# Normalised units of an FFN in small tiles, the row factor half a unit sooner, recurrence constants in the mixer

## The chip, the cores and the metric

The kernel runs on one core of a Trainium2 chip. The metric is the device time of one execution in microseconds (us). Before the change it is 1784.41 us, the median of three runs (1784.16 to 1784.74). A measurement of this kernel repeats to about a tenth of a per cent.

## What is computed

One decoder layer on x of 256 rows (SEQ) by 2048 columns (D_MODEL), in fp32; D_FF is 5632. Two half-step SwiGLU FFNs stand around a token mixer:

```python
def swiglu_ffn(x, w_gate, w_up, w_down):
    return (jax.nn.silu(x @ w_gate) * (x @ w_up)) @ w_down
...
x = x + 0.5 * swiglu_ffn(rms_norm(x, ffn1_norm), ffn1_w_gate, ffn1_w_up, ffn1_w_down)
z = rms_norm(x, mix_norm) @ w_in
...                                  # conv and RG-LRU with a GELU gate; gated short conv
x = x + y @ w_out                    # y: both branches, each RMS-normalised
x = x + 0.5 * swiglu_ffn(rms_norm(x, ffn2_norm), ffn2_w_gate, ffn2_w_up, ffn2_w_down)
return rms_norm(x, final_norm)
```

Of the recurrence only one thing matters here: it needs a vector worked out from the weights alone, a multiple of softplus(-lambda), and halves of two bias vectors.

## The kernel before

**Numbers.** An fp32 product is made of fp32r parts. A tile is split into hi (a cast by ScalarE) and lo (the tile less hi, by VectorE), and TensorE adds hi by hi, lo by hi and hi by lo in PSUM. So each weight tile of 512 rows by 512 columns (in SBUF 128 partitions by 2048) is loaded by SyncE's queue (`load`, L155, its DMA at L164), cast in two pieces of 1024 and subtracted in one of 2048 (`parts_of`, L169), and then multiplied (`multiply`, L194). In `multiply` the products with the hi part of the weights come first, those with lo last. Raw tiles come from the pool `raws` (three buffers) or, with `kept`, from a pool of the FFN in which the tag "kept" has two buffers. All compute is recorded through the class `Engine` (L42), so the profile puts it all under L42, and tiles are told apart by name.

**x.** The rows stay in SBUF as `xres` (two row halves t = 0, 1 of 128 rows). `Norm` (L207) turns x into `xT`, four units u of 512 columns each (the k of a product), with gain and hi/lo parts, but without the factor of each row. `factor` (L237) takes 1/sqrt of the mean square of each row; `rows` (L243) makes of it a tile `bc`, the factor along the free axis, by two matmuls (`pb`) of ones with a diagonal matrix `diag`, for which there is one buffer.

**An FFN** (`ffn`, L383). Its first 512 columns of gate and up are done with the unnormalised units (loop at L443: u = 0 to 3, for each first gate, then up; weights `raw_g` and `raw_u` by name, sums in `ps_g` and `ps_u`), and the row factor is put on afterwards, when `sg` is made (L485 to 488). In the first FFN (`opening`) the transposes of x stand in the same loop, and up to u = 1 the order of each engine is the order in which the code is written (`Engine.pinned`); everywhere else a scheduler orders the instructions of each engine.

In the same loop stand the factor (L473), the rows (L475) and the normalising of the units (L476 to 482). `normalise(u)` (L421) adds the parts of a unit, multiplies by bc into an fp32 copy `v`, casts it to hi and subtracts for lo, giving `x` of that unit (x_0 to x_3 in the text). The copies v of all four units lie in the two "kept" buffers (L417, L418). When unit 1 is done, `seven_of` (L308) makes the sums and differences of blocks of v that the seven-product passes need (tiles `spare` and `xs`).

After that five pairs of 512-column blocks follow (L531), for each pair a gate pass and an up pass (`seven`, L326). Such a pass takes the 2 by 2 blocks of units 0 and 1 with seven products instead of eight (12 matmuls of 512 columns each, `product_of`) and units 2 and 3 in the usual way (`usual`, four blocks of 24 matmuls): 180 matmuls. The first products are product 0 (weight w11 alone, into `ps_g_a`) and product 4 (w12 - w11, into `ps_g_c`, stationary side `xs`); the sum of product 4 is then copied by ScalarE (`s5`), units 2 and 3 go on into the same sum and into `ps_g_e`. Both w11 and w12 are loaded into "kept" buffers (L336). Eight transposes of `sg` (`ph`) stand in the gate pass. After pairs 0, 2 and 4 the down products follow (L493). Tiles of 512 columns that live for a while (`spare`, `sg`, `s1`, `s5` and the like) come from a tag "keep" with 13 buffers (L390).

**Between the FFNs.** In the first FFN `prepare` (L566) is called at L491: it turns the small vectors (gains, biases, convolution weights, lambda) with two transposes (`pv_many`, `pv_conv`) and works out the recurrence's constants with an Abs and an Exp on ScalarE and 25 small VectorE steps (`lam_...`). The mixer (L605) walks through ten blocks of 512 columns of w_in (order at L782, weights `raw_in`, sums `ps_in`) and does its elementwise work piece by piece beside them: `defer` (L59) queues a piece, `pump` (L66) takes some behind each unit. Then comes the product with w_out (L803, weights `raw_o`), and the second FFN.

Of the kernel before, what the change touches and what calls it, by code (L numbers as in the profile page):

```python
# [10 lines left out]
F32 = mybir.dt.float32  # L11
F32R = mybir.dt.float32r
AF = mybir.ActivationFunctionType
ALU = mybir.AluOpType
AX = mybir.AxisListType

P = 128
D = 2048
S = 256
FF = 5632  # L20
NT = S // P
# [4 lines left out]
UK = 4  # L26
# [22 lines left out]
def hybrid_block(ctx: ExitStack, tc: tile.TileContext, a: dict, out: bass.AP):  # L49
    nc = tc.nc  # L50
    Engine.pinned = False
    dve, act, pe = (Engine(tc, e) for e in (nc.vector, nc.scalar, nc.tensor))
    x = a["x"][0]
# [5 lines left out]
    def defer(cost, fn):  # L59
        pending.append((cost, fn))  # L60
# [23 lines left out]
    def f32(ap):  # L84
        return ap.bitcast(F32)
# [104 lines left out]
    def stationary(tile, t):  # L190

        return [(tile[:, j, t * P : (t + 1) * P], tile[:, j, S + t * P : S + (t + 1) * P]) for j in range(UK)]
# [14 lines left out]
    class Norm:  # L207
# [35 lines left out]
        def rows(self):  # L243

            pb = bank(f"pb_{self.name}")
            for t in range(NT):
                dg = work.tile([P, P], F32, tag="diag", name=f"diag_{self.name}_{t}", bufs=1)
                dve.tensor_scalar(dg, ident, self.r[:, t : t + 1], None, op0=ALU.mult)
                pe.matmul(pb[:, t * P : (t + 1) * P], ones, dg, start=True, stop=True)
            self.bc = work.tile([P, S], F32, tag="bc", name=f"bc_{self.name}")  # L250
            dve.tensor_copy(self.bc, pb[:, :S])
# [71 lines left out]
    def quad(tile):  # L323
        return tile.rearrange("p (j c) -> p j c", j=UK)
# [58 lines left out]
    def ffn(tag, norm, after, opening=False):  # L383
        with tc.tile_pool(name=f"ffn{tag}", bufs=1) as fp:
# [29 lines left out]
                    turn_hidden(*waiting.pop(0))  # L414


            vs = [fp.tile([P, UK, 2, S], F32, tag="kept", name=f"v{tag}_{i}", bufs=2) for i in range(2)]  # L417
            vs = [vs[u // 2][:, :, u % 2, :] for u in range(4)]  # L418
            xs, sf = [], {}

            def normalise(u):  # L421

                bcs = norm.bc.unsqueeze(1).to_broadcast([P, UK, S])
                x = f32(norm.xT[u])
                dve.tensor_tensor(vs[u], x[:, :, :S], x[:, :, S:], op=ALU.add)
                dve.tensor_tensor(vs[u], vs[u], bcs, op=ALU.mult)
                xs.append(big(f"x{tag}_{u}"))
                act.copy(xs[u][:, :, :S], vs[u])
                dve.tensor_tensor(xs[u][:, :, S:], vs[u], f32(xs[u][:, :, :S]), op=ALU.subtract)
                if u == 1:  # L430
                    pair = [big(f"xs{tag}_{i}") for i in range(2)]
                    sf.update(
                        seven_of(
                            xs[0], xs[1],
                            {(t, i): vs[i][:, :, t * P : (t + 1) * P] for t in range(NT) for i in range(2)},
                            quad(keep(f"spare{tag}")),
                            [(b[:, :, o : o + P], b[:, :, o + P : o + S]) for b in pair for o in (0, S)],
                        )
                    )
# [3 lines left out]
            for u in range(KD // UK):  # L443
                for m, w in (("g", wg), ("u", wu)):
                    n = f"{m}{tag}_0_{u}"
                    src = w[u * UK * P : (u + 1) * UK * P, :CW]
                    if opening and (u, m) == (0, "g"):
                        pieces = ((0, 1), (1, 2), (2, 4))
                        raw = load(src, n, pieces, lambda i: load_x(1) if i == 1 else None)
                        blk = parts_of(raw, n, pieces, lambda i: norm.turn((i,) if i < 2 else (2, 3)))  # L450
                        for j in range(UK):
                            for t in range(NT):
                                yh, yl = stationary(norm.xT[u], t)[j]
                                pe.matmul(ps[m, t], yh, blk[j][0], start=j == 0, stop=False)
                                pe.matmul(ps[m, t], yl, blk[j][0], start=False, stop=False)
                                pe.matmul(ps[m, t], yh, blk[j][1], start=False, stop=False)
                        continue
                    raw = load(src, n)
                    if opening and u < 2 and m == "u":
                        load_x(u + 2)  # L460
                    blk = parts_of(raw, n, ((0, 2), (2, 4)), (lambda i: None) if opening else None)
                    if opening and u < 3 and m == "u":
                        norm.turn(range(4 * u + 4, 4 * u + 8))
                        if u == 0:
                            norm.squares(0)
                        norm.squares(u + 1)
                    multiply([(ps[m, t], stationary(norm.xT[u], t), u == 0, u == 3) for t in range(NT)], blk)
                    pump(1.5)
                    if (u, m) == (1, "u"):
                        Engine.pinned = False  # L470
                        flush()
                    elif (u, m) == (2, "u") and opening or (u, m) == (2, "g") and not opening:
                        norm.factor()  # L473
                    elif (u, m) == (3, "g") and opening or (u, m) == (2, "u"):
                        norm.rows()  # L475
                        normalise(0)  # L476
                    if u == 3:
                        for k in range(len(xs), len(xs) + 2):
                            if k < 4:
                                normalise(k)  # L480
            for k in range(len(xs), 4):
                normalise(k)
            xs = list(enumerate(xs))[2:]
# [3 lines left out]
                dve.scalar_tensor_tensor(sg, ps["u", t], norm.r[:, t : t + 1], sg, op0=ALU.mult, op1=ALU.mult)  # L487
                waiting.append((0, t, sg, False))
            turn_of["hold"] = False
            if tag == 1:  # L490
                prepare()  # L491

            def down(last):  # L493
                us = sorted(set(hidden) | {w[0] for w in waiting})
# [36 lines left out]
            for s in range(5):  # L531
                cs = (CW + 2 * s * CW, 2 * CW + 2 * s * CW)
                sg = {}

                def total(ps, tiles):
                    for p in tiles[1:]:
                        dve.tensor_tensor(tiles[0], tiles[0], p, op=ALU.add)
                    if not tiles:
                        return ps
                    dve.tensor_tensor(tiles[0], ps, tiles[0], op=ALU.add)  # L540
                    return tiles[0]

                def gate(t, n, ps, tiles):
                    g = total(ps, tiles)
                    sg[t, n] = tiles[0] if tiles else keep(f"z{tag}_{s}")
                    act.activation(sg[t, n], g, AF.Silu)

                def up(t, n, ps, tiles):
                    dve.tensor_tensor(sg[t, n], total(ps, tiles), sg[t, n], op=ALU.mult)
                    if (t, n) == (1, 0):  # L550
                        settle()
                    waiting.append((1 + 2 * s + n, t, sg[t, n], s % 2 == 0))

                seven(wg, (0, 1), cs, sf, xs, f"g{tag}_{s}", keep, gate, settle)
                seven(wu, (0, 1), cs, sf, xs, f"u{tag}_{s}", keep, up)
                if s % 2 == 0:
                    down(s == 4)
            extra.clear()


# [3 lines left out]
    sp2, hba, hbi = small("sp2"), small("hba"), small("hbi")  # L564

    def prepare():  # L566
        for t in turns:
            t()

        lam = vec["lru_lambda"]  # L570
        m, e, den, sr, s2, pl = (small(f"lam_{n}") for n in ("abs", "exp", "den", "s", "s2", "poly"))
        act.activation(m, lam, AF.Abs)
        act.activation(e, m, AF.Exp, scale=-1.0)
        dve.tensor_scalar(den, e, 2.0, None, op0=ALU.add)
        dve.reciprocal(den, den)
        dve.tensor_tensor(sr, e, den, op=ALU.mult)
        dve.tensor_tensor(s2, sr, sr, op=ALU.mult)
        dve.tensor_scalar(pl, s2, 2.0 / 17, 2.0 / 15, op0=ALU.mult, op1=ALU.add)
        for d in (13, 11, 9, 7, 5, 3, 1):
            dve.tensor_tensor(pl, pl, s2, op=ALU.mult)  # L580
            dve.tensor_scalar(pl, pl, 2.0 / d, None, op0=ALU.add)
        dve.tensor_tensor(pl, pl, sr, op=ALU.mult)
        dve.tensor_scalar(sp2, lam, -1.0, 0.0, op0=ALU.mult, op1=ALU.max)
        dve.tensor_tensor(sp2, sp2, pl, op=ALU.add)
        dve.tensor_scalar(sp2, sp2, 2.0, None, op0=ALU.mult)
        dve.tensor_scalar(hba, vec["lru_b_a"], 0.5, None, op0=ALU.mult)
        dve.tensor_scalar(hbi, vec["lru_b_i"], 0.5, None, op0=ALU.mult)
# [17 lines left out]
    with tc.tile_pool(name="mixer", bufs=1) as mp, tc.tile_pool(name="mixw", bufs=2) as mw:  # L605
# [165 lines left out]
        def sc_b(ps, half):  # L771
            if any(4 * half + f not in ys for f in range(4)):
                flush()
            for f in range(4):
# [4 lines left out]
                dve.tensor_tensor(y, b, y, op=ALU.mult)  # L779
                defer(0.8, lambda q=q, y=y: finish(y, NH + q, vec["sc_out_norm"][:, q : q + 1], 1, q == 0))  # L780

        order = [  # L782
            (lru_x, 0, 0), (lru_x, 0, 1), (sc_c, 3, 0), (lru_gate, 1, 0), (sc_x, 4, 0),
            (lru_gate, 1, 1), (sc_c, 3, 1), (sc_x, 4, 1), (sc_b, 2, 0), (sc_b, 2, 1),
# [116 lines left out]
```

## Time and profile before

| what | us |
|---|---|
| median of three runs | 1784.41 |
| the profiled execution, its own time | 1786.55 |
| its span in the profile | 1784.7 |
| TensorE (PE) busy | 1740.5 (98%) |
| VectorE (DVE) busy | 1494.5 (84%) |
| ScalarE (ACT) busy | 1047.0 (59%) |

The profiled execution is one of its own, longer than its span by 1.85 us, and the medians come from other runs. In rows of the timeline, the first number is the start within the span and the second the duration in us (of all instructions of the row together, whose number is at the end, x8); then come engine, line, operation, out<-in, and in brackets the idle time of the engine before it, with what ended that. A row of an `SPq` lists issues of the DMA queue. A row of a stretch gives from:to and its length, then busy time and, in brackets, the number of instructions of TensorE's matmuls, TensorE's weight loads, VectorE, ScalarE and GpSimd, and behind them the granted clock of TensorE (1 is full), the share of DMA and GB/s.

### The profile page before, as it was taken

What the parts mean: (1) busy time and instruction counts of PE and PEld (TensorE: products, weight loads), DVE (VectorE), ACT (ScalarE), POOL (GpSimd) and SP (SyncE); (2) the same over time, 40 slices, a digit from 0 to 9 for tenths busy, and PEclk for the clock granted to TensorE, in tenths of its full rate; (3) what the DMA queues carried; (4) which work ended last, traced back from release to release, by engine and by line L of the source; (5) the groups of instructions that cost most, each with busy time, mean ns of one, the idle gap of its engine ahead of it and who ended that gap; (6) DMA issues with size and microseconds to landing.
All of it is one profiled execution on the core that took longest, in us unless ns stands there. A gap on an engine that the chain in (4) does not pass through costs nothing. (4 is left out here: it accounts for less than half of the span.)

```text
span 1784.7 us, 20306 instructions
## 1 busy us (share of the span) xinstructions
PE 1740.5 (98%) x8031; PEld 1439.8 (81%) x8031; DVE 1494.5 (84%) x1228; ACT 1047.0 (59%) x1342; POOL 6.9 (0%) x32
## 2 busy tenths in 40 slices
PE   8699999999999999999999998999999999999998
PEld 7488788888888888888888886788788888888886
DVE  7798989989789888588987666989899887899895
ACT  6465566665466656565765453665466554566654
POOL 1000000000000000000000000000000000000000
PEclk9899999999999999999999999999999999999999
DMA  8266555574565564555555564564566647555652
GB/s 286 93 208 217 207 194 189 189 240 166 184 205 196 190 234 167 164 188 190 176 186 194 199 204 151 188 224 138 203 216 204 202 158 259 188 189 189 236 179 105
DMA packets 173904, 343.24 MB, mean 192 GB/s; under 512 B 5620, under 2 KB 8048, under 8 KB 173680
## 3 DMA queue, kind: packets, MB, share of 16 engines
q1 hardware_dynamic: 173344, 340.82, 56.9%
q8 instruction: 63, 1.03, 0.2%
q10 hardware_dynamic: 144, 1.05, 0.1%
q14 instruction: 33, 0.27, 0.0%
q0 software_dynamic: 320, 0.07, 0.0%
HBM read 339.82 MB, written 2.10 MB: 192 GB/s over the span
## 5 line engine op out<-in xcount | busy, mean ns | idle before, releaser
L42 PE MATMUL ps_in<-xT_nm,hi_in 128*128 128x512 f32 x640 | 222.9, 393 | 0.0
L42 ACT CAST hi_g_p<-raw_g 128x1024 fp32r<-128x1024 f32 x140 | 142.2, 1049 | 110.6 <-DVE raw_g L42 46.1
L42 DVE TENSOR_TENSOR lo_g_p<-raw_g,hi_g_p 128x2048 fp32r<-128x2048 f32 x70 | 159.7, 2287 | 42.1 <-ACT hi_g_p L42 40.9
L42 ACT CAST hi_u_p<-raw_u 128x1024 fp32r<-128x1024 f32 x140 | 141.3, 1049 | 70.9 <-PE ps_u_a L42 25.7
L42 PE MATMUL ps_in<-xT_nm,lo_in 128*128 128x256 f32 x640 | 178.5, 280 | 0.7 <-DVE lo_in L42 0.7
L42 DVE TENSOR_TENSOR lo_u_p<-raw_u,hi_u_p 128x2048 fp32r<-128x2048 f32 x70 | 159.1, 2286 | 20.3 <-ACT hi_u_p L42 20.1
L42 PE MATMUL ps_d<-hi_d,h 128*128 128x512 f32 x704 | 169.6, 392 | 0.0
L42 PEld LDWEIGHTS ps_d<-hi_d,h 128*128 128x128 f32 x704 | 131.5, 188 | 28.2
L42 PEld LDWEIGHTS ps_in<-xT_nm,hi_in 128*128 128x128 f32 x640 | 119.6, 187 | 26.0
L42 ACT CAST hi_d<-raw_d 128x1024 fp32r<-128x1024 f32 x88 | 88.2, 1049 | 69.2 <-PE ps_u_d L42 22.7
L42 DVE TENSOR_TENSOR lo_d<-raw_d,hi_d 128x2048 fp32r<-128x2048 f32 x44 | 100.6, 2290 | 33.3 <-ACT hi_d L42 33.3
L42 PEld LDWEIGHTS ps_in<-xT_nm,lo_in 128*128 128x128 f32 x640 | 120.6, 189 | 1.6 <-DVE lo_in L42 1.5
L42 DVE TENSOR_TENSOR lo_in<-raw_in,hi_in 128x2048 fp32r<-128x2048 f32 x40 | 91.3, 2284 | 32.5 <-ACT hi_in L42 32.3
L42 ACT CAST hi_in<-raw_in 128x1024 fp32r<-128x1024 f32 x80 | 81.5, 1049 | 61.8 <-PE ps_in L42 48.5
L42 ACT CAST hi_d_p<-raw_d 128x1024 fp32r<-128x1024 f32 x84 | 84.4, 1048 | 56.4 <-DVE raw_d L42 32.9
L42 DVE TENSOR_TENSOR lo_d_p<-raw_d,hi_d_p 128x2048 fp32r<-128x2048 f32 x42 | 95.5, 2287 | 18.0 <-ACT hi_d_p L42 17.9
L42 ACT CAST hi_g_x<-raw_g 128x1024 fp32r<-128x1024 f32 x80 | 81.2, 1049 | 41.6 <-PE ps_g_c L42 22.9
L42 ACT CAST hi_u_x<-raw_u 128x1024 fp32r<-128x1024 f32 x80 | 80.6, 1049 | 37.2 <-PE ps_u_c L42 25.5
L42 DVE TENSOR_TENSOR raw_u<-raw_u,raw_u 128x2048 f32<-128x2048 f32 x40 | 91.6, 2290 | 10.1 <-DMA raw_u<-in_ffn_w_up_dram 9.5
L42 DVE TENSOR_TENSOR raw_g<-raw_g,raw_g 128x2048 f32<-128x2048 f32 x40 | 91.4, 2287 | 7.0 <-DMA raw_g<-in_ffn_w_gate_dram 6.5
L42 DVE TENSOR_TENSOR lo_g_x<-raw_g,hi_g_x 128x2048 fp32r<-128x2048 f32 x40 | 91.4, 2284 | 2.3 <-ACT hi_g_x L42 2.1
L42 DVE TENSOR_TENSOR lo_u_x<-raw_u,hi_u_x 128x2048 fp32r<-128x2048 f32 x40 | 91.4, 2285 | 0.9 <-ACT hi_u_x L42 0.2
(348 smaller groups left out, 3606.9 us busy)
## 6 DMA issues: line engine op xcount, KB each, us to landing
raw_u<-in_ffn_w_up_dram SPq DMA_DIRECT2D x88, 1024.0 KB, 5.2
raw_d<-in_ffn_w_down_dram SPq DMA_DIRECT2D x88, 1024.0 KB, 5.2
raw_g<-in_ffn_w_gate_dram SPq DMA_DIRECT2D x87, 1024.0 KB, 5.3
raw_in<-in_w_in_dram SPq DMA_DIRECT2D x40, 1024.0 KB, 5.1
raw_o<-in_w_out_dram SPq DMA_DIRECT2D x16, 1024.0 KB, 5.1
xres<-in_x_dram SPq DMA_DIRECT2D x4, 512.0 KB, 8.2
fin<-in_final_norm_dram ACTq DMA_DIRECT2D x1, 1024.0 KB, 5.6
out_dram<-xres SPq DMA_DIRECT2D x4, 256.0 KB, 2.7
```

The costliest lines, as they stand in the source:

```text
L42: ins = getattr(self.engine, name)(*args, **kwargs)
```

## The change

Three things, which the diff shows whole.

1. The copies v of the normalised units leave the two "kept" buffers. Each unit and row half has a tile of 512 columns of its own with tag "keep" (eight of its 13 buffers). `normalise` works row half by row half: add, multiply, cast and subtract each take 512 columns twice where they took 1024 once. The "kept" buffers hold nothing but raw weights.
2. The row factor: `diag` has two buffers (the pool's default) instead of one. In the first FFN `factor` is called ahead of up unit 2's products instead of behind them, and `rows` and the normalising of unit 0 behind up unit 2 instead of behind gate unit 3. In the second FFN `factor` is called behind up unit 1 instead of gate unit 2, and `rows` and the normalising of unit 0 behind gate unit 2 instead of up unit 2.
3. `prepare` is not called in the first FFN but queued ahead of the mixer's loop. The two transposes of the small vectors, which stood in it, come behind the up pass of the first FFN's pair s = 1.

```diff
@@ class Norm, rows
-                dg = work.tile([P, P], F32, tag="diag", name=f"diag_{self.name}_{t}", bufs=1)
+                dg = work.tile([P, P], F32, tag="diag", name=f"diag_{self.name}_{t}")
@@ ffn
-            vs = [fp.tile([P, UK, 2, S], F32, tag="kept", name=f"v{tag}_{i}", bufs=2) for i in range(2)]
-            vs = [vs[u // 2][:, :, u % 2, :] for u in range(4)]
-            xs, sf = [], {}
+            xs, vs, sf = [], {}, {}
 
             def normalise(u):
 
-                bcs = norm.bc.unsqueeze(1).to_broadcast([P, UK, S])
-                x = f32(norm.xT[u])
-                dve.tensor_tensor(vs[u], x[:, :, :S], x[:, :, S:], op=ALU.add)
-                dve.tensor_tensor(vs[u], vs[u], bcs, op=ALU.mult)
                 xs.append(big(f"x{tag}_{u}"))
-                act.copy(xs[u][:, :, :S], vs[u])
-                dve.tensor_tensor(xs[u][:, :, S:], vs[u], f32(xs[u][:, :, :S]), op=ALU.subtract)
+                for t in range(NT):
+                    hi, lo = (slice(o + t * P, o + (t + 1) * P) for o in (0, S))
+                    v = vs[t, u] = quad(keep(f"v{tag}_{u}_{t}"))
+                    x = f32(norm.xT[u])
+                    dve.tensor_tensor(v, x[:, :, hi], x[:, :, lo], op=ALU.add)
+                    dve.tensor_tensor(v, v, norm.bc[:, hi].unsqueeze(1).to_broadcast([P, UK, P]), op=ALU.mult)
+                    act.copy(xs[u][:, :, hi], v)
+                    dve.tensor_tensor(xs[u][:, :, lo], v, f32(xs[u][:, :, hi]), op=ALU.subtract)
                 if u == 1:
                     pair = [big(f"xs{tag}_{i}") for i in range(2)]
                     sf.update(
                         seven_of(
                             xs[0], xs[1],
-                            {(t, i): vs[i][:, :, t * P : (t + 1) * P] for t in range(NT) for i in range(2)},
+                            vs,
...
+                        if u == 2:
+                            norm.factor()
                     multiply([(ps[m, t], stationary(norm.xT[u], t), u == 0, u == 3) for t in range(NT)], blk)
                     pump(1.5)
                     if (u, m) == (1, "u"):
                         Engine.pinned = False
                         flush()
-                    elif (u, m) == (2, "u") and opening or (u, m) == (2, "g") and not opening:
-                        norm.factor()
-                    elif (u, m) == (3, "g") and opening or (u, m) == (2, "u"):
+                        if not opening:
+                            norm.factor()
+                    elif (u, m) == (2, "u" if opening else "g"):
                         norm.rows()
                         normalise(0)
...
             turn_of["hold"] = False
-            if tag == 1:
-                prepare()
@@ ffn, loop over s
                 if s % 2 == 0:
                     down(s == 4)
+                elif s == 1 and tag == 1:
+                    for t in turns:
+                        t()
@@ prepare
-        for t in turns:
-            t()
@@ mixer
+        defer(5.0, prepare)
         order = [
```

## The prediction

> **What bounds the kernel now.** The page first, part 2, the clock that TensorE was granted in 40 slices:
>
> ```profile
> PEclk9899999999999999999999999999999999999999
> ```
>
> The chain that ended last is TensorE work, at full clock nearly everywhere. So what counts is where TensorE stands still. The list of its waits (total, times, longest):
>
> ```profile
> PE ps_g_a L42 <- ACT hi_g_p L42: 23.4, 3, 15.0
> PE ps_g_c L42 <- ACT hi_g_p L42: 3.9, 2, 2.1
> ```
>
> 27.3 us go to two tiles, ps_g_a and ps_g_c: the first products of the first seven-product pass of each FFN. TensorE's timeline shows both places (start, duration; the bracket is the idle time before). FFN 1's first gate pass lies between pv_many, which takes the place right behind the last ps_u, and ps_u_a:
>
> ```profile
> 56.66 0.23 PE L42 MATMUL pv_many<-ident,rows_many 80*128 80x80 f32 x1
> ...
> 72.06 3.78 PE L42 MATMUL ps_g_a<-hi_g_p,x 128*128 128x512 f32 x8 [14.97 <-ACT hi_g_p L42]
> ...
> 78.87 3.54 PE L42 MATMUL ps_g_c<-hi_g_p,xs 128*128 128x512 f32 x8 [2.07 <-ACT hi_g_p L42]
> ...
> 120.08 1.98 PE L42 MATMUL ps_u_a<-hi_u_p,x 128*128 128x512 f32 x8
> ```
>
> ```profile
> 1102.55 1.98 PE L42 MATMUL ps_u<-lo_u,xT_n 128*128 128x512 f32 x8
> 1112.70 3.78 PE L42 MATMUL ps_g_a<-hi_g_p,x 128*128 128x512 f32 x8 [8.17 <-ACT hi_g_p L42]
> 1116.28 1.35 PE L42 MATMUL ps_g_a<-lo_g_p,x 128*128 128x512 f32 x4
> 1119.43 3.11 PE L42 MATMUL ps_g_c<-hi_g_p,xs 128*128 128x512 f32 x8 [1.80 <-ACT hi_g_p L42]
> ```
>
> Who is late behind hi_g_p? ScalarE's cast waits for a transfer, and SyncE's issues tell since when:
>
> ```profile
> 70.96 1.99 ACT L42 CAST hi_g_p<-raw_g 128x1024 fp32r<-128x1024 f32 x2 [1.44 <-DMA raw_g<-in_ffn_w_gate_dram]
> ```
>
> ```profile
> 65.84 24.80 SPq L164 DMA_DIRECT2D raw_g<-in_ffn_w_gate_dram  x4
> ```
>
> ```profile
> 1106.47 18.89 SPq L164 DMA_DIRECT2D raw_g<-in_ffn_w_gate_dram  x3
> ```
>
> ```profile
> raw_g<-in_ffn_w_gate_dram SPq DMA_DIRECT2D x87, 1024.0 KB, 5.3
> ```
>
> The weight tile w11 takes a "kept" buffer, and both of these hold the units' fp32 copies until the last is normalised. Its load starts only at 65.84 and 1106.47, takes about 5.3 us (the page's part 6), and the cast follows: normalising, load and cast stand in a row.
>
> A smaller cost is the clock, in stretches of 1 us (the third number from the end):
>
> ```profile
> 62.00:63.00 1.00, 0.00 (x0) 0.00 (x0) 1.00 (x3) 1.00 (x3) 0.00 (x0) 0.56 0.00 0
> 75.00:76.00 1.00, 1.00 (x4) 0.61 (x4) 1.00 (x3) 0.00 (x0) 0.00 (x0) 0.61 0.00 0
> 79.00:80.00 1.00, 1.00 (x3) 0.82 (x4) 1.00 (x2) 1.00 (x2) 0.00 (x0) 0.59 0.00 0
> 82.00:83.00 1.00, 1.00 (x4) 0.78 (x4) 1.00 (x3) 0.56 (x1) 0.00 (x0) 0.70 0.00 0
> ```
>
> TensorE idle from 57 falls to half clock within 62 to 63, is back within 75 to 76, and falls again at about 79.4 after the idle 2.07 us, for some 3.2 us.
>
> A dense pass prices the loss. From the chain of waits:
>
> ```profile
> 1500.36 21.95 PE ps_d L42 x96
> ```
>
> 21.95 / 96 = 0.2286 us per matmul. A first pass has 180 of them (seven products of 12, four usual blocks of 24) and 8 transposes with a quarter of the columns (0.8 us, an estimate between 8 x 0.06 and 8 x 0.23): 41.9 us. FFN 1 took 120.08 - 56.66 = 63.4, a loss of **21.5** (14.97 + 2.07 of waits, the rest clock).
>
> **The change part by part.** VectorE sets the new times, so its rows:
>
> ```profile
> 50.98 0.29 DVE L42 TENSOR_SCALAR diag_n<-ident,r_n 128x128 f32<-128x128 f32 x1 [6.98 <-PE pb_n L42]
> 51.85 0.43 DVE L42 COPY bc_n<-pb_n 128x256 f32<-128x256 f32 x1 [0.58 <-PE pb_n L42]
> ```
>
> ```profile
> 62.80 1.28 DVE L42 TENSOR_TENSOR xs<-v,xs 128x512 fp32r<-128x512 f32 x2
> ```
>
> ```profile
> 91.28 6.69 DVE L42 TENSOR_TENSOR lo_g_p<-raw_g,hi_g_p 128x2048 fp32r<-128x2048 f32 x3 [1.07 <-ACT hi_g_p L42]
> ```
>
> ```profile
> 1087.71 2.29 DVE L42 TENSOR_TENSOR lo_u<-raw_u,hi_u 128x2048 fp32r<-128x2048 f32 x1 [3.15 <-ACT hi_u L42]
> ```
>
> ```profile
> 1094.09 0.42 DVE L42 COPY bc_n<-pb_n 128x256 f32<-128x256 f32 x1 [0.58 <-PE pb_n L42]
> ```
>
> ```profile
> 1115.95 4.62 DVE L42 TENSOR_TENSOR raw_g<-raw_g,raw_g 128x2048 f32<-128x2048 f32 x2
> ```
>
> Steps back to back: 2048 columns 2.20 us (6.69 for three, the last shown with its latency of 0.09); 512 columns, of which two take 1.28 with the same tail, 0.60 us.
>
> *FFN 1.* Gate unit 3 follows up unit 2 on TensorE here:
>
> ```profile
> 45.07 3.84 PE L42 MATMUL ps_g<-hi_g,xT_n 128*128 128x512 f32 x16
> ```
>
> The order of the changed program puts w11's load before that of the third up unit and w12's behind the last, so both lie ready. diag's second buffer ends the 6.98 us wait, and the factor's matmuls pb move to 45.07, ahead of this row. VectorE then takes (order of the changed program, waits named there): lo of w11, which needs the buffer that up unit 2 reads until then; bc; the subtraction w12 - w11; then 512-column pieces, with lo of that difference behind the seventh. Starting at 45.5 (the cast and up unit 2's last read):
> - x_0 is complete after 2 x 2.20 + 0.35 (bc) + 5 x 0.60 = 7.8: 53.3, and TensorE is in up unit 3 until 56.66. The 14.97 us go.
> - xs_0 (product 4) is complete after 3 x 2.20 + 0.35 + 12 x 0.60 = 14.2: 59.7. TensorE's ps_g_a ends at 56.66 + 12 x 0.2286 = 59.4. **Wait 0.3.**
> - x_2's second half comes after 24 small pieces: 45.5 + 6.6 + 0.35 + 14.4 = 66.9; ps_g_c ends at 62.5. **Wait 4.4: this is what is late next.**
> - ps_g_c's next matmuls need s5, which ScalarE copies behind x_2, a table load, x_3 and both sg. Its rows:
>
> ```profile
> 55.77 1.28 ACT L42 ACT_TABLE_LOAD   x1
> 57.06 0.69 ACT L42 ACTIVATE sg<-ps_g,r_n 128x512 f32<-128x512 f32 x1
> 58.71 0.62 ACT L42 CAST xs<-spare 128x512 fp32r<-128x512 f32 x1 [0.96 <-DVE spare L42]
> ```
>
>   From x_2's cast, about 65.8: + 1.28 + two sg and four pieces of about 0.55 to 0.65 = 70.4; TensorE is there at 69.2. **Wait 1.2.**
> - lo of the first usual block: 72.8 against 72.6, **0.2**. Then 140 matmuls, 32.0 us, with VectorE still behind by some 1.5 us near 90 (seven more steps of 2048 and two small to lo of product 6): ps_u_a starts near 72.8 + 32.0 + 1.5 = 106.3 against 120.08, **-13.8 at full clock**. Clock: the 4.4 us wait must still cost some. TensorE lost some 4.4 us to it before (21.5 - 17.04); between nothing and that I take 1.8, as a dip here lies in part beside the waits of 1.2 and 1.5: **-12.0** (-14 to -9.5).
>
> *FFN 2.* w11 and w12 are loaded during the output projection. Here the order puts all of the normalising ahead of lo of w11. lo_u at 1087.71, bc at 1089.9 (before: 1094.09), then 28 pieces of 0.60 and the two sg of 0.62: 1108.4; lo of w11 until 1110.7. TensorE does the 8 hi matmuls from 1102.55 + 8 x 0.2286 = 1104.4, ends at 1106.2, and **waits 4.5 us**; before, VectorE was there at 1115.9. The subtraction (2.2) and half a cast (1.0) follow: ps_g_c at 1114.1 against 1119.43, **-5.3**. From there the same order as before, with the same kind of dip in clock; -6.5 to -3, I take **-4.8**.
>
> *Smaller parts.* Splitting 1024 into 2 x 512 adds 24 x 0.60 - 12 x 1.14 = 0.7 us of VectorE per FFN; it is in the counts. The kept pool holds 13: eight copies, spare, two sg, s1, s5 fill it exactly, and the next takes a copy long read. SyncE: in the opening w11 passes three loads. Their cover:
>
> ```profile
> 29.37 1.06 ACT L42 CAST hi_u<-raw_u 128x1024 fp32r<-128x1024 f32 x1
> ```
>
> ```profile
> 39.48 3.92 PE L42 MATMUL ps_u<-hi_u,xT_n 128*128 128x512 f32 x16
> ```
>
> Cast 10 us before use, so 5.3 us more would be hidden; without that cover it would cost 5.3. In the output projection w11 waits for the last reader of the mixer's tiles, the small products of the row sums in column block 0; the w_out loads stand behind it, but at that point they run three ahead. I take 0 (bounds 0 to 5.3).
>
> *Mixer and constants.* pv_many and pv_conv, some 0.3 us, leave an idle place of TensorE for a busy one. The 25 small VectorE steps and the Exp with its table load go into a later, dense gate pass; its table load, 1.28 us, comes with another back.
>
> ```profile
> L42 DVE TENSOR_TENSOR lam_poly<-lam_poly,lam_s 128x8 f32<-128x8 f32 x8 | 1.3, 166 | 0.2
> ```
>
> ```profile
> 720.00:980.00 260.00, 258.83 (x1478) 226.19 (x1477) 208.66 (x303) 157.41 (x260) 1.05 (x16) 1.00 0.55 180
> ```
>
> 25 x 0.166 = 4.2 us; VectorE's free time in that pass hides them, as they step in beside the large ones (an uncovered one costs its 0.166, so up to 4.2). In the mixer the scheduler has dealt VectorE's small steps out anew. TensorE stood still for 260 - 258.83 = 1.2 us there; it may be 0 to 4. Both together: -1.2 to +4, I take **+1.3**.
>
> **Sum:** -12.0 - 4.8 + 1.3 = **-15.5**.
>
> ```profile
> span 1784.7 us, 20306 instructions
> ```
>
> The profiled execution took 1786.55 us, 1.85 around its span; it becomes 1771.05. The median shown is 1784.41: 1784.41 - 15.5 = **1768.9, so 1769.0**.
>
> **The rivals.**
> 1. *Both passes run dense.* FFN 1 gains its 21.5, FFN 2 its 8.17 + 1.80 and about 4 of clock, 14: 1749. For: the loads are off the path. Against: VectorE's count of 24 and 28 pieces. 3 in 100.
> 2. *The mixer gives half back.* VectorE has 208.66 of 260 us there; where a weight's lo of 2.29 us slips behind four more small steps, TensorE waits 1 to 2 us. Five such: +8, 1777. For: new order. Against: 1.2 us of waits before, with the same work. 12 in 100.
> 3. *Slower, by the clock.* Waits of 4.4, 1.2 and 1.5 us spread over FFN 1's gate pass could keep TensorE at half clock, not just dip it. Price 0.2286 per matmul. Whole pass at half clock: 180 x 0.2286 = +41 against -15.5: 1810. It decides from 68 matmuls more at half clock than now. For: half clock followed even a gap of 2.07 us. Against: some 3.5 us of work restored the clock at 75 to 76, and 16 us without a wait follow 72.8. 6 in 100. [...]
> 4. *The copies were not what held the load*, nothing changes: 1784.4. Against: the SyncE rows start right when normalising ends. 3 in 100.
>
> **How the numbers follow.** Forecast 76 in 100, with its own range of 1763 to 1775 (terms at their ends, -21.7 to -8.5 together, not all at once). The range reaches on to rival 2: 1763 to 1777. A measurement here tells 0.2%, 3.6 us, from no change. Faster by more: forecast, rivals 1 and 2, 0.91; within: 0.03; slower: 0.06.
>
> **What would show it.** Right: ps_g_a starts within 0.5 us of the last ps_u in FFN 1; the longest wait there stands before ps_g_e on x, 3.5 to 5.5 us; in FFN 2 the wait stands within ps_g_a, before its lo matmuls, on VectorE, 3.5 to 5.5 us; ps_u_a starts 10 to 14 us earlier in FFN 1. Wrong: a wait for a DMA of raw_g or raw_o at either place, waits over 3 us in the mixer, or half clock beyond 10 us in either pass.

## The result, and the profile after

| | median, us | runs | against before |
|---|---|---|---|
| before, same chip | 1784.58 | 1784.16 to 1786.13 | |
| changed kernel | 1773.18 | 1770.94 to 1773.95 | ratio 0.9932, 95% interval 0.9915 to 0.9950 |
| changed kernel, later series | 1772.84 | 1768.30 to 1775.44 | 0.9920, 0.9907 to 0.9934 (before there 1786.31) |

The medians differ by 11.4 and 13.5 us; the two intervals reach from 8.9 to 16.6. The forecast was 15.5 faster, 1769.0, with a range of 1763 to 1777: both medians lie within the range, and both are smaller gains than the forecast. The profiled execution of the changed kernel took 1770.94, the shortest of its four runs; its span is 1769.0, 15.7 under the span before. Runs spread more than the tenth of a per cent named at the start: the changed kernel's by 0.4% in the later series, those of the kernel before by 0.4% (1783.72 to 1790.64, 17 runs) in the longest one.

The granted clock of the page of the changed kernel, and TensorE's longest waits (the two left out, pt_n and pv_first, stand at the very start, before and after alike; the list goes on with waits of 0.9 us and less):

```profile
PEclk9999999999999999999999999999999999999999
```

```profile
PE ps_g_a L42 <- DVE lo_g_p L42: 4.7, 1, 4.7
PE ps_g_e L42 <- ACT x L42: 3.4, 1, 3.4
...
PE ps_g_c L42 <- ACT hi_g_p L42: 1.6, 1, 1.6
PE ps_in L42 <- DVE lo_in L42: 1.6, 3, 0.9
```

The 8 in the second slice is gone, and so are the 23.4 us that ps_g_a waited behind hi_g_p; 4.7 us behind VectorE (FFN 2) and 3.4 on x (FFN 1) stand in their place. FFN 1's head, the stretch from the last products of `ps_u` to ps_u_a, on TensorE's timeline of the changed kernel:

```profile
54.49 1.98 PE L42 MATMUL ps_u<-lo_u,xT_n 128*128 128x512 f32 x8
56.30 2.01 PE L42 MATMUL ps_g_a<-hi_g_p,x 128*128 128x512 f32 x8
...
59.63 1.90 PE L42 MATMUL ps_g_c<-hi_g_p,xs 128*128 128x512 f32 x7 [0.17 <-DVE xs L42]
...
65.82 0.49 PE L42 MATMUL ps_g_e<-hi_g_x,x 128*128 128x512 f32 x1 [3.35 <-ACT x L42]
66.97 3.36 PE L42 MATMUL ps_g_e<-hi_g_x,x 128*128 128x512 f32 x7 [0.66 <-DVE x L42]
...
92.06 2.12 PE L42 MATMUL ps_g_a<-hi_g_x,x 128*128 128x512 f32 x8 [0.94 <-ACT u_g L42]
...
106.83 1.98 PE L42 MATMUL ps_u_a<-hi_u_p,x 128*128 128x512 f32 x8
```

ps_g_a follows up unit 3 at once; the wait is at ps_g_e, on the two halves of x_2: 3.35 + 0.66 = 4.0 us. ps_u_a starts 13.25 us sooner (106.83 against 120.08). FFN 2's head:

```profile
1092.85 1.98 PE L42 MATMUL ps_u<-lo_u,xT_n 128*128 128x512 f32 x8
1094.66 2.01 PE L42 MATMUL ps_g_a<-hi_g_p,x 128*128 128x512 f32 x8
1101.40 2.07 PE L42 MATMUL ps_g_a<-lo_g_p,x 128*128 128x512 f32 x4 [4.73 <-DVE lo_g_p L42]
1105.10 3.42 PE L42 MATMUL ps_g_c<-hi_g_p,xs 128*128 128x512 f32 x8 [1.62 <-ACT hi_g_p L42]
...
1145.87 1.98 PE L42 MATMUL ps_u_a<-hi_u_p,x 128*128 128x512 f32 x8
```

The end of this head before the change:

```profile
1160.47 0.84 PE L42 MATMUL ps_u_a<-hi_u_p,x 128*128 128x512 f32 x3
```

The wait stands within ps_g_a, ahead of its lo products. The last ps_u is 9.70 sooner than before, ps_u_a 14.60. So between the two heads 13.25 - 9.70 = 3.55 us were given back, the head of FFN 2 gained 4.90, and what lies behind it 1.1 more. Most of what was given back is in the mixer; the rows of ps_in (first and last start), before and after:

```profile
L42 PE MATMUL ps_in<-xT_nm,hi_in x640: 391/391/481, 737.0 to 968.0; 128*128 128x512 f32 x160
```

```profile
L42 PE MATMUL ps_in<-xT_nm,hi_in x640: 387/395/503, 724.3 to 958.5; 128*128 128x512 f32 x160
```

231.0 us became 234.2.

What sets the two heads now is told by the stretches of the changed kernel (columns as before: TensorE, weight loads, VectorE third):

```profile
45.40:100.40 55.00, 49.77 (x211) 38.98 (x210) 54.66 (x52) 34.93 (x45) 0.00 (x0) 0.97 0.40 134
1061.70:1078.20 16.50, 16.50 (x77) 13.62 (x75) 6.88 (x3) 6.05 (x7) 0.00 (x0) 1.00 0.54 172
1078.20:1118.20 40.00, 33.65 (x142) 26.75 (x142) 39.85 (x42) 23.30 (x31) 0.00 (x0) 0.91 0.23 69
```

VectorE is busy 54.66 of 55 us and 39.85 of 40, while in the 16.5 us ahead of FFN 2's head it works 6.88. The two heads differ in one thing: in FFN 1 VectorE stays busy to the end of the first gate pass (60.99 us of the 61.4 from 45.4 to 106.8), in FFN 2 for its first half only (27.56 of 27.65 from 1092.85 to 1120.5, then 22.07 of 25.3). What follows from VectorE's load is the experiments' question.

### The profile page after: what moved, and what is told of

It reads as the page before. It is cut to its first block, busy times and chain, and to the rows that moved or that the text cites. A ratio compares the mean times of both kernels' runs of the same rounds, so it can differ in the third digit from the quotient of the medians.

```text
span 1769.0 us, 20338 instructions
## 1 busy us (share of the span) xinstructions
PE 1739.7 (98%) x8031; PEld 1436.8 (81%) x8031; DVE 1495.7 (85%) x1252; ACT 1047.6 (59%) x1350; POOL 7.0 (0%) x32
```

## The experiments

The kernel before was run beside each on the same chip: 1786.31 us beside the first three rows of this table, 1785.13 beside now, x2_first, lo_first and early, 1785.97 beside the others. These are three chips, so kernels of different rows are compared by their ratios.

| kernel | median, us | ratio to before, 95% interval |
|---|---|---|
| small tiles alone (tiles) | 1775.68 | 0.9942, 0.9928 to 0.9956 |
| factor alone (factor) | 1773.58 | 0.9926, 0.9914 to 0.9939 |
| both, constants as before (tiles_factor) | 1772.29 | 0.9924, 0.9911 to 0.9936 |
| changed, constants not queued (now) | 1770.27 | 0.9916, 0.9902 to 0.9930 |
| changed, x_2 ahead of three sums (x2_first) | 1771.47 | 0.9920, 0.9907 to 0.9932 |
| changed, lo of w11 first in FFN 2 (lo_first) | 1768.26 | 0.9904, 0.9890 to 0.9918 |
| changed, FFN 2's factor earlier (early) | 1764.55 | 0.9881, 0.9868 to 0.9894 |
| constants alone (const) | 1788.14 | 1.0009, 1.0000 to 1.0017 |
| changed, 21 matmuls of no use (fill) | 1772.00 | 0.9921, 0.9908 to 0.9933 |
| early and now together (early_now) | 1763.09 | 0.9870, 0.9857 to 0.9883 |
| that and 15 matmuls of no use (early_now_fill) | 1761.65 | 0.9861, 0.9848 to 0.9874 |

### Which part brings the gain

The edits are the parts of the diff above, each alone on the kernel before. **Small tiles alone:**

> Part 1 alone: small tiles for the normalised copies, factor, rows and constants where they were before. Theory A (the two parts stand in for each other: the load behind the kept buffers and the late start of normalising end in the same wait, so either one alone brings most of the gain): -8 to -11 us against before, no wait for a transfer of raw_g at the first ps_g_a of either FFN, and waits on x or xs of ScalarE and VectorE in their place. Theory B (the parts add up, and the factor given out half a unit, 5.5 us of TensorE work, sooner is worth about that in each FFN): about -2 to -5.

Measured -10.6 us. TensorE's timeline of this kernel, FFN 1:

```profile
59.14 0.50 PE L42 MATMUL ps_g_a<-hi_g_p,x 128*128 128x512 f32 x1 [1.56 <-ACT x L42]
...
72.34 3.93 PE L42 MATMUL ps_g_e<-hi_g_x,x 128*128 128x512 f32 x8 [2.17 <-ACT x L42]
```

The load is gone from the path, and normalising is what is waited for. **The factor alone:**

> Part 2 alone: factor, rows and diag as in the change, the copies still in the kept buffers. Theory A: normalising starts some 5 to 7 us sooner and with it the load of w11 in both FFNs, so the wait ahead of ps_g_a is 7 to 8.5 us in FFN 1 (before 14.97) and 3.5 to 4.5 in FFN 2 (before 8.17): -9 to -12 us. Theory B (the small tiles are what brings the gain, the factor alone little): -2 to -5.

Measured -12.7, a little more than theory A's -9 to -12. Its timeline, FFN 1:

```profile
65.20 3.78 PE L42 MATMUL ps_g_a<-hi_g_p,x 128*128 128x512 f32 x8 [7.62 <-ACT hi_g_p L42]
```

The copies still hold w11's buffer and the wait of 14.97 is 7.62, as expected. **Both:**

> Parts 1 and 2 without part 3: the vectors are turned and the constants made in the first FFN as before. Theory M (the mixer's extra 3.1 us, 724.30 to 958.85 against 736.95 to 968.37, come from part 3, by the new order of VectorE's steps or by what follows from it): the mixer takes 231 to 232 us as before, and the kernel is 2 to 4 us faster than the changed one. Rival R (the mixer's pace is not set by part 3; TensorE falls into a slower or a faster rhythm of its own, 353 or 347 ns for a pair of ps_in matmuls in the two traces, whatever the kernel): mixer anywhere from 231 to 235, total within 1.5 us of the changed kernel.

Measured -14.0. The two parts alone would add up to 23.3 and bring 14.0 together: theory A, they stand in for each other, and theory B is out. The small tiles add 1.3 us at most to what the earlier factor brings by itself, less than these runs can tell.

The mixer here is back at 230.5 us (727.5 to 958.0 in the row of ps_in), which is 230.9 as the expectation counts it, up to the first ps_o, and near the 231 to 232 of theory M; but the total is not 2 to 4 us under the changed kernel (0.9924 against 0.9920 and 0.9932). FFN 1 and TensorE's wait in the up pass behind it:

```profile
68.58 3.78 PE L42 MATMUL ps_g_e<-hi_g_x,x 128*128 128x512 f32 x8 [5.37 <-ACT sg L42]
...
108.53 1.98 PE L42 MATMUL ps_u_a<-hi_u_p,x 128*128 128x512 f32 x8
```

```profile
PE ps_u_c L42 <- DVE lo_u_p L42: 1.2, 1, 1.2
```

VectorE makes the constants here from 79.9 to 107.5, in a stretch where it is busy nearly all the time (59.1 us of the 62 from 45 to 107). From ps_u_a to the first ps_in it takes 618.96 us against 617.5 in both traces of the changed kernel, with this wait of 1.2 us for VectorE's lo in it: some 1.5 of the 3.7 to 4.2 us that the mixer saves are lost there. ps_u_a itself is later too (108.53 against 106.83 and, below, 107.53), but that can't be put down to the constants: five kernels further on (now, lo_first, early, fill, early_now) have the changed kernel's code in this pass and come to 107.8 to 108.6. So theory M is right about the mixer and wrong about the total, and where all of the difference goes isn't shown.

**The changed kernel again:**

> The changed kernel once more, for its interval and for a second trace. By the sum of the profile rows (-13.3 in the first gate pass of FFN 1, +0.6 at its third pair, +3.1 in the mixer, -5.1 in FFN 2's first gate pass, -1.1 in the two behind it) -15.7 us; by the medians of the four runs so far -11.4. If the trace differs in the mixer's rhythm or in the stretches at half clock, that accounts for runs 2 to 3 us apart; if it is the same to 0.2 us, it is not the kernel's own work that varies.

Its span is 1771.7, 2.7 more than in the first trace. ps_u_a of FFN 1 starts at 107.53 (0.7 later), the mixer takes 234.7 (725.0 to 959.7 in the row of ps_in), and FFN 2's head 54.3 from the last ps_u instead of 53.0:

```profile
1094.05 1.98 PE L42 MATMUL ps_u<-lo_u,xT_n 128*128 128x512 f32 x8
...
1102.61 2.08 PE L42 MATMUL ps_g_a<-lo_g_p,x 128*128 128x512 f32 x4 [4.74 <-DVE lo_g_p L42]
...
1148.39 1.98 PE L42 MATMUL ps_u_a<-hi_u_p,x 128*128 128x512 f32 x8
```

The wait is the same to 0.01 us, the stretch at half clock is longer, 10.2 us against 6.8: the clock rows of the two traces, of 1110 to 1111 us, first trace and second:

```profile
1110.00:1111.00 1.00, 1.00 (x7) 0.80 (x6) 1.00 (x2) 0.59 (x2) 0.00 (x0) 1.00 0.00 0
```

```profile
1110.00:1111.00 1.00, 1.00 (x4) 0.81 (x3) 1.00 (x1) 0.88 (x1) 0.00 (x0) 0.50 0.00 0
```

So the same program differs by some 3 us, and the sum of one trace's rows (-15.7; by the second trace -13.0) is one draw of it.

### What ends the heads: VectorE's order or its total

x2_first records normalise(2) (`between`) behind the sum for product 4 and ahead of the other three (`sums`), in `seven_of`, for both FFNs:

```diff
...
+            if i == 5 and between:
+                between()
+                sums()
             act.copy(hi, q)
...
```

> The changed kernel with another order of VectorE's work in both heads: of the sums for products 4, 5, 6 and 2 only that of product 4 is made ahead of unit 2's normalising, the other three behind it. Theory V (VectorE's total work up to product 6 sets the end of the head; its order only decides before which product TensorE waits): the wait of 3.35 + 0.66 on x in FFN 1 goes, as large a one (3 to 6 us) stands at another place, on lo of a weight, and ps_u_a of FFN 1 comes within 0.7 us of 107; total within 1.5 us of the changed kernel. Rival O (x_2's second half is late by its order alone, the sums have time): ps_u_a of FFN 1 3 to 4 us sooner, total -3 to -6 against the changed kernel.

```profile
62.76 2.29 PE L42 MATMUL ps_g_e<-hi_g_x,x 128*128 128x512 f32 x8
70.26 1.22 PE L42 MATMUL ps_g_e<-lo_g_x,x 128*128 128x512 f32 x2 [5.21 <-DVE lo_g_x L42]
...
106.95 1.98 PE L42 MATMUL ps_u_a<-hi_u_p,x 128*128 128x512 f32 x8
```

x_2 is there in time, and TensorE waits 5.21 us eight matmuls later, for lo of the same block's weight. ps_u_a starts at 106.95 (106.83 and 107.53 in the two traces of the changed kernel): theory V. The order of VectorE's work in FFN 1 moves the wait and does not shorten the pass. In FFN 2, too, the waits change places (1.6 us within ps_g_a and 5.3 at ps_g_c, where it was 4.7 and 1.6), and the pass from ps_g_a to ps_u_a takes 51.9 us, between the 51.2 and 52.5 of the changed kernel.

lo_first records w11's load, cast and lo ahead of units 1 to 3, in FFN 2:

```diff
...
+                    if tag == 2 and (u, m) == (3, "g"):
+                        first = [
+                            load(wg[:UK * P, o : o + CW], f"g{tag}_0_0{i}", kept=True)
+                            for i, o in enumerate((CW, 2 * CW))
+                        ]
+                        first.append(parts_of(first[0], f"g{tag}_0_p0"))
                     if u == 3:
                         for k in range(len(xs), len(xs) + 2):
...
```

> The changed kernel, in FFN 2 with w11's load, cast and lo recorded ahead of the normalising of units 1 to 3, so VectorE makes that lo before them. Theory V (VectorE's total): the wait of 4.7 within ps_g_a goes and returns in smaller ones behind, 2.5 to 4.5 together; what is saved is the time at half clock (two to three stretches of 3.4 us at half) more than the wait: first gate pass of FFN 2 (ps_g_a to ps_u_a) 47 to 50 us against 51.21 and 52.53; total -2 to -5. Rival O (only the place of the one lo is wrong): all 4.7 + 1.6 us and the clock, pass at 42 to 44, total -8 to -10.

From ps_g_a to ps_u_a it takes 47.87 us (1096.38 to 1144.24), inside what theory V gave, and the total is -16.9 to before against -11.4 and -13.5. The intervals of the ratios overlap (0.9890 to 0.9918 against 0.9907 to 0.9934), so the total leans that way and no more. The wait of 4.7 is gone, and smaller ones follow it, 2.7 us in all instead of 6.3, the largest:

```profile
1104.80 1.19 PE L42 MATMUL ps_g_c<-lo_g_p,xs 128*128 128x512 f32 x4 [0.92 <-DVE lo_g_p L42]
```

One stretch of 3.4 us at half clock is left, where the two traces of the changed kernel have 6.8 and 10.2 us. So here, where VectorE's load ends halfway through the pass, another order alone shortens it by 3.3 and 4.7 us, unlike in FFN 1.

early lets VectorE begin where it is idle (`flush`, which records what is still queued, moves along with the factor):

```diff
...
+                    elif (u, m) == (0, "u") and not opening:
+                        flush()
+                        norm.factor()
-                    elif (u, m) == (2, "u" if opening else "g"):
+                    elif (u, m) == ((2, "u") if opening else (1, "g")):
                         norm.rows()
                         normalise(0)
+                    elif (u, m) in ((1, "u"), (2, "g")) and not opening:
+                        normalise(len(xs))
...
```

> The changed kernel, in FFN 2 with the row factor behind up unit 0 instead of up unit 1, and rows and the normalising of units 0, 1 and 2 behind gate 1, up 1 and gate 2. VectorE is idle 3.2 us ahead of each lo_u and lo_g there (1062 to 1078), some 12 us. Theory V (VectorE's total work behind the row factor sets the end of the head, so an earlier factor, which lets its idle time be used, moves it): no wait over 1.5 us in the head of FFN 2, no half clock there, pass at 42 to 44 against 51.21 and 52.53: total -7 to -10 against the changed kernel. Rival L (something else ends there, the cast of w11 or its load): pass over 48, total within 3 us.

```profile
1093.45 2.01 PE L42 MATMUL ps_g_a<-hi_g_p,x 128*128 128x512 f32 x8
1095.30 1.08 PE L42 MATMUL ps_g_a<-lo_g_p,x 128*128 128x512 f32 x4
1096.22 2.01 PE L42 MATMUL ps_g_c<-hi_g_p,xs 128*128 128x512 f32 x8
...
1136.97 1.98 PE L42 MATMUL ps_u_a<-hi_u_p,x 128*128 128x512 f32 x8
```

```profile
1060.50:1077.00 16.50, 16.50 (x76) 13.64 (x75) 13.22 (x17) 8.34 (x13) 0.00 (x0) 1.00 0.44 143
1077.00:1117.00 40.00, 39.25 (x174) 31.49 (x173) 39.25 (x32) 25.04 (x32) 0.00 (x0) 1.00 0.38 122
```

The pass takes 43.5 us instead of 51.2 and 52.5, at full clock (1.00 up to 1117). VectorE works 13.22 us of the 16.5 ahead of the head, where it worked 6.88, and TensorE 39.25 of the 40 behind. The rival (load or cast of w11) is out: neither was touched, and the pass is not over 48. This is the largest step beyond the changed kernel by one edit, 0.9881 against 0.9920 and 0.9932, and the intervals don't touch (0.9868 to 0.9894, 0.9907 to 0.9934).

### The half clock

fill adds matmuls of no use to the wait of 4.7 us:

```diff
...
+        for i in range(fill[0]):
+            pe.matmul(c, sf[0][i % UK][0], blk[i % UK][0], start=True, stop=True, skip_group_check=True)
...
```

(16 in FFN 2's first gate pass, between hi and lo of product 0, and five behind lo, which the scheduler puts in the same place).

> The changed kernel with 21 matmuls more in FFN 2's first gate pass, between the hi and the lo products of product 0, where TensorE waits 4.7 us for VectorE; they go into ps_g_c, which product 4 starts anew, so nothing is computed with them. VectorE's work is the same. Theory H (an idle TensorE pays twice, by the wait and by two or three stretches of 3.4 us at half clock behind it): no half clock in FFN 2's head or one stretch less, pass 49 to 51 against 51.21 and 52.53, total -1 to -3 although 21 matmuls were added. Rival V' (VectorE sets the pace behind the wait, so a faster TensorE only waits more): pass 51 to 53, total within 1 us of the changed kernel.

```profile
1098.04 4.97 PE L42 MATMUL ps_g_c<-hi_g_p,x 128*128 128x512 f32 x21
1102.93 1.21 PE L42 MATMUL ps_g_a<-lo_g_p,x 128*128 128x512 f32 x4
1106.39 3.30 PE L42 MATMUL ps_g_c<-hi_g_p,xs 128*128 128x512 f32 x8 [2.25 <-ACT hi_g_p L42]
```

The clock is full until 1107.0, and half (0.50) for one stretch of 3.4 us behind the remaining wait of 2.25 us, where the two traces of the changed kernel have 6.8 and 10.2 us. The pass takes 51.3 us, not 49 to 51, and the total is 0.9921: rival V', or too little for theory H to be seen. In FFN 1, with early_now as the base, the same was done at the wait on x:

> As the one before, with 15 matmuls more that compute nothing in FFN 1's first gate pass, in the wait on x (into ps_g_e, which the next block starts anew). Theory H: no half clock in FFN 1 (before 3.4 to 6.8 us of it), ps_u_a of FFN 1 at 104.5 to 106 against 106.8 to 108.6, total -1 to -3 against the kernel without them. Rival V': ps_u_a as without, the waits behind grow by as much.

```profile
66.28 0.50 PE L42 MATMUL ps_g_e<-hi_g_x,x 128*128 128x512 f32 x1 [0.28 <-ACT x L42]
67.44 1.88 PE L42 MATMUL ps_g_e<-hi_g_x,x 128*128 128x512 f32 x7 [0.65 <-DVE x L42]
...
70.86 2.12 PE L42 MATMUL ps_g_c<-hi_g_x,x 128*128 128x512 f32 x8 [0.90 <-ACT s_g L42]
...
107.13 1.98 PE L42 MATMUL ps_u_a<-hi_u_p,x 128*128 128x512 f32 x8
```

No half clock is left in FFN 1, where early_now has 6.8 us of it, worth 3.4 us of work. ps_u_a starts at 107.13 instead of 108.25, and a new wait of 0.90 stands at ps_g_c. The start alone tells little, as traces with the changed kernel's code in this pass have it at 106.8 to 108.6; the length of the pass, from ps_g_a to ps_u_a, tells more. It is 50.25 us without half clock, 50.5 in both traces of the changed kernel with 3.4 us of it, and 51.3 to 51.7 in the five (now, lo_first, early, fill, early_now) with 6.8. So 6.8 us at half clock, worth 3.4 us of work, cost 1.0 to 1.4 us here, and most of that comes with the second 3.4. Neither theory's numbers hold: behind a wait for VectorE the half clock costs less than half of its face value here. The pass without half clock is one trace. The totals, 1761.65 (1759.41 to 1763.14) and 1763.09 (1762.73 to 1763.58), are too near each other to tell.

What brings half clock on and how long it holds, these traces don't settle. The dip of fill in FFN 2's head came after 2.25 us of idle time, and one of the kernel before, near 79, after 2.07. Behind the same wait of 4.73 and 4.74 us, two traces of one program have 6.8 and 10.2 us of half clock.

### What the constants cost

const is part 3 alone:

> Part 3 alone on the kernel before. Theory D (part 3's price is the mixer's queue, whatever stands ahead of it): the mixer 234 to 235.5 us against 231.42, ps_u_a of FFN 1 within 0.5 us of 120 (its wait for w11 covers the constants either way), +0.6 at the third pair: +2.5 to +5 against before. Rival (part 3 has no price of its own; the mixer was slow in the changed kernel because of what came before it): mixer 231 to 232, total within 1 us of before.

Measured +2.2 us, at the limit of what can be told (1.0000 to 1.0017) and a little under theory D's +2.5 to +5; the mixer takes 234.0 (737.6 to 971.6 in the row of ps_in), as theory D says and not as its rival does. now takes the queueing away:

```diff
-        defer(5.0, prepare)
+        prepare()
```

> The changed kernel, but the recurrence's constants are recorded directly ahead of the mixer's loop instead of being queued with a cost of 5.0; their instructions stay the same and stand in the same third pair of FFN 1. Theory D (the queue's debt: the piece of cost 5.0 uses up what the next products would have taken, so that all later deferred work of the mixer comes some three products later and VectorE's steps are dealt out anew): the mixer takes 231 to 232 us instead of 234.54 and 235.05, total 2 to 4 us under the changed kernel. Rival C (the constants' own 25 steps and the moved vectors are what costs): mixer 234 to 235, total as the changed kernel within 1 us.

```profile
L42 PE MATMUL ps_in<-xT_nm,hi_in x640: 387/391/478, 726.1 to 956.6; 128*128 128x512 f32 x160
```

The constants' steps are the same and stand in the same pass, and the mixer takes 230.5 us, as theory D says. The total doesn't tell: -14.9 against before, where the changed kernel has -11.4 and -13.5, with intervals that overlap. The reason that theory D gives is read from the code: `pump` subtracts 5.0 from a budget that gets 1.5 per unit, and carries the debt, so that all deferred work of the mixer comes later. The expectations count the mixer up to the first ps_o, 0.4 us more than these rows. Over all traces of the study: with the queued constants 234.2, 234.7, 234.0, 231.9, 234.6, 232.0, 234.6 (mean 233.7), without them 231.0, 232.6, 231.0, 230.5, 230.5, 232.4, 232.6 (mean 231.5). So the queued constants cost 2.2 us on average, and the changed kernel's own trace had 0.5 more than the mean. But the two groups overlap (231.9 and 232.0 with, 232.4 and 232.6 without), so one pair of traces can't show it. What goes with a long mixer in the traces is TensorE's waits for hi_in and lo_in: none in now and tiles_factor (230.5 both), 1.1 us in early and x2_first (232.0 and 231.9), 1.8 and 2.4 in the two traces of the changed kernel (234.2 and 234.7). That the debt is what makes those tiles late is argued and not shown.

**Both mends:**

> Both mends together: FFN 2's factor and normalising earlier, and the constants recorded ahead of the mixer's loop. If they are independent places, their traces add up: FFN 2's pass 43.5 as in the one, mixer 230.9 as in the other, total 10 to 13 us under the changed kernel and 23 to 27 under before. If the mixer's pace comes from somewhere else, mixer 232 to 235 and total 8 to 10 under the changed kernel.

FFN 2's pass takes 43.5 us as with early, but the mixer takes 232.4 and not the 230.5 of now, no less than the 232.0 of early with the queue. The total is 22.9 under before, 9.4 and 11.5 more than the changed kernel's two. The second forecast (mixer 232 to 235, 8 to 10) is met at least as well as the first, so the two mends do not simply add up, and the step from early (0.9881) to early_now (0.9870) is within the intervals. With the 15 matmuls of no use it is 24.3 under before, the lowest median here (0.9861). Both beat the kernel before and the changed one.

## Why the prediction was right, point by point

| step | forecast | first trace | second trace |
|---|---|---|---|
| FFN 1, ps_u_a | -12.0 (-14 to -9.5) | -13.25 | -12.55 |
| FFN 2, last ps_u to ps_u_a | -4.8 (-6.5 to -3) | -4.90 | -3.58 |
| between them: mixer, constants | +1.3 (-1.2 to +4) | +3.55 | +4.05 |
| behind FFN 2's head | 0 | -1.1 | -0.9 |
| sum | -15.5 | -15.7 | -13.0 |

That the first trace comes within 0.2 us of the forecast is luck: FFN 1 and the stretch behind FFN 2's head gave 2.35 us more than forecast, and what lies between the heads gave 2.25 back. In the second trace FFN 2 falls short as well, by 1.2. The places and the mechanism are what was right.

- **The load off the path: right.** ps_g_a follows ps_u in both FFNs without a wait for a transfer.
- **What is late next in FFN 1: right in place and size.** 0.3 forecast at ps_g_c and 0.17 found, 4.4 on x_2 and 4.0 found, 1.5 near 90 and 0.94 found (there the trace names ScalarE, which had itself waited 2.54 us for VectorE's lo). The 1.2 on s5 did not come; TensorE was still at half clock and later there.
- **Why it is late: too narrow.** The prediction gave VectorE's order piece by piece and named x_2. x2_first shows that in FFN 1 not the order but VectorE's total sets the end; the forecast held because the count of pieces did. In FFN 2 the order counts as well (lo_first).
- **FFN 2: right,** 4.5 forecast within ps_g_a and 4.73 found. In the second trace the wait is the same (4.74), but the head gains 3.58 instead of 4.90, because half clock lasts 10.2 us there instead of 6.8. What was not seen: VectorE's idle time ahead of it (6.88 of 16.5 us used), worth more than what the change won in that head.
- **Clock:** 1.8 taken in FFN 1 behind the wait. One stretch of 3.4 us came in each of the two traces, 1.7 us of work, but 6.8 us in five other kernels with the same code there; by the lengths of the pass the 3.4 us cost 0.3 us and the 6.8 us 1.0 to 1.4. So the term was too large. In FFN 2 the second trace has 10.2 us at half clock, over the 10 that the prediction named as a sign of being wrong.
- **Mixer and constants: the term that was mis-sized.** The steps of the constants in a dense pass and the vectors' turns were small, as forecast (ps_u_a to the first ps_in 617.48 us against 616.88, +0.6). But of the +1.3 that leaves 0.7 for the mixer's new order, and it was +3.1 (+3.6 in the second trace). The prediction took the new order for a matter of chance with bounds of 0 to 4 us of waits. The traces with and without the queue point at a likely cause, the queue's debt, that stood in the diff: a cost of 5.0 in a budget of 1.5 per unit.
- **Rivals.** 1 (dense) was wrong for FFN 1 by VectorE's count; early makes it nearly true for FFN 2 (43.5 us for the pass, 41.9 for a dense one by the prediction's count). 2 (the mixer gives half back) came in part: 3.1 of the 8 it named. 3 (half clock throughout) did not come: 3.4 us of half clock in FFN 1, 6.8 and 10.2 in FFN 2, and in the first trace none behind them until the last 5.7 us of the span. 4 is out.

## What to carry to other kernels

Two waits in a row behind one late step are not two gains: ask what one engine has to do between the latest event that starts it and the first product that needs all of it, and count that engine's work, whichever buffer the trace names as releaser. Where that engine is busy to the end of the stretch, as VectorE in FFN 1, another order only moved the wait to another tile (ps_u_a at 106.95 against 106.83 and 107.53). Where it is busy for the first half only, as in FFN 2, another order shortened the pass (47.9 us against 51.2 and 52.5), and an earlier start into the engine's idle time shortened it more (43.5). And where work is dealt out by budgets, look at the declared cost of a new piece too, not only at its instructions.

## What the runs showed of the hardware

**TensorE kept two paces at full clock in the mixer.** A pair of matmuls (512 columns, then 256) repeats there in a fixed rhythm. TensorE's timeline before, the first and the 65th pair of a run of them:

```profile
901.45 0.39 PE L42 MATMUL ps_in<-xT_nm,hi_in 128*128 128x512 f32 x1
...
923.63 0.39 PE L42 MATMUL ps_in<-xT_nm,hi_in 128*128 128x512 f32 x1
```

and of the changed kernel:

```profile
891.00 0.40 PE L42 MATMUL ps_in<-xT_nm,hi_in 128*128 128x512 f32 x1
...
913.63 0.40 PE L42 MATMUL ps_in<-xT_nm,hi_in 128*128 128x512 f32 x1
```

22.18 us and 22.63 for 64 pairs, 346.6 and 353.6 ns each, no wait in either and the clock at 1.00. Here the slower rhythm begins behind a wait of 0.93 us for a lo_in and holds for some 80 us, to the end of the mixer. In now, which waits nowhere in the mixer, the slower rhythm occurs too (15 pairs from 726.09 to 731.37, 352.0 ns each), so it doesn't take such a wait. Both paces occur in the mixer of the kernel before as well: some 353 ns in its first 4 us and from about 215 us on, 346 to 347 for most of what lies between. What makes the pace isn't shown; 2% of the mixer is at stake.

**The same program's mixer differs by up to 2.7 us.** The traces of early and of the changed kernel have the same mixer: 232.0 and 234.2, 234.7. They part some 24 us into it, at a load of w_in: ScalarE's timeline of early, and of the changed kernel's second trace:

```profile
743.53 2.00 ACT L42 CAST hi_in<-raw_in 128x1024 fp32r<-128x1024 f32 x2 [1.68 <-DMA raw_in<-in_w_in_dram]
```

```profile
745.61 2.00 ACT L42 CAST hi_in<-raw_in 128x1024 fp32r<-128x1024 f32 x2 [3.85 <-DMA raw_in<-in_w_in_dram]
```

The first ps_in was at 725.3 and 725.0, and the cast that waits for the transfer starts 2.1 us later. TensorE then waits 0.99 and 0.31 us for two lo tiles, where early doesn't wait: 1.3 of the 2.7. Without any of their waits the two mixers still differ by 1.4 us (234.7 - 2.4 and 232.0 - 1.1). The changed kernel's first trace keeps the slower rhythm (353 ns) from about 70 to 120 us into the mixer; at the faster pace that would be about 1 us shorter. Why the transfer is later, and whether the rhythm has to do with it, was not tried.
